# Attention's value products with V stationary, two heads on the two column halves of the array, scaled once per token tile

## The chip, the cores and the metric

The kernel runs on one core of a Trainium2 chip. The metric is the device time of one execution in microseconds (us), the median of several runs. One execution was also recorded by the hardware profiler. The engines are TensorE (PE in the rows; its weight loads PEld), VectorE (DVE), ScalarE (ACT), GpSimd (POOL) and the queue of SyncE (SP), which issues the loads.

## What is computed

Two layers of a diffusion backbone over 256 context tokens and 512 latent tokens of width 1024. Each layer projects the modulated input once, runs three mixers side by side (a gated MLP over tokens, grouped-query attention, a gated DeltaNet in both directions), joins them in one output projection with a post-norm, and ends with a squared-ReLU MLP. The change is in attention: 6 query heads of 64 channels share 2 key and value heads, a latent token sees all 768 tokens, a context token the 256 of the context, and the second layer needs only the latent tokens.

```
def _attend(q, k, v):
    s = jnp.einsum('bqhgd,bkhd->bhgqk', q, k).astype(jnp.float32) * (HEAD_DIM ** -0.5)
    pr = jax.nn.softmax(s, axis=-1).astype(v.dtype)
    return jnp.einsum('bhgqk,bkhd->bqhgd', pr, v)
```

## The kernel before

The kernel is written as streams of steps (Python generators). A planner (`Flow`, with a rough cost of each instruction in `Flow.cost`) decides at build time which stream goes on next; the engines then run what was traced in that order, each engine in order. Every operation is recorded by one helper, so all rows carry line 206, and tiles are told apart by their names.

A layer has three stages. First come the projections: q, k, v for attention, the convolutions of the DeltaNet, the gate z (`z_gate`, which shares the one buffer `axn` with `qk_norm`). Then, in one call of `flow.run`, attention runs beside the DeltaNet: three pairs of heads, each with a chain of 12 scan steps (`dn_scan`: products with `rW`, `rT`, `rK`, then `rQ` and `rA` for the output; each step ends a copy `vn` on ACT), the making of their operands (`gs`, `rW`, `rK`, ...), and the preparation of the third pair (`Lx`, `Xx`, `tm` on DVE). The chains have a head start of 1000 ns (`BIAS`) in the planner's choice, so that attention fills the gaps between their steps. In the first layer `mods` also streams the next modulation weights (`modw`) through PE in this stage. At the end come the output projection (`y`, `yh`, `whi`) and the MLP. The output projection starts after attention in program order, and for each token tile it needs all mixers.

Attention (`attention`, `att_out`) goes over token tiles t of 128 (6 in the first layer, 4 in the second) and 6 heads in each. For a head: the scores are four products of the queries `qs` with the key parts `akh` and `akl` (two for a context tile) into a wide PSUM tile `ax`; DVE takes the row maximum `amx` and scales it to `anm`; ACT takes the exponential `ape` with its row sum, DVE the reciprocal `ars`; PE transposes `ape` in blocks of 128 keys, ACT copies them to `apT`; and for each block of 128 keys c one product with `apT` stationary and the values of both value heads moving adds to a PSUM tile of 128 columns, of which the head uses 64. DVE scales these by `ars` into `aot`. After the sixth head three transposes of `aot` and a copy `ayb` on ACT make the tile channel-major, and ACT's queue issues its store. A head has 6 blocks of keys in a latent tile and 2 in a context tile: 312 products in all, 168 in the first layer and 144 in the second. The scores of a head are traced ahead of the products of the head before.

PSUM tiles are lent out by the planner: four narrow ones of one bank (`mm`) and two wide ones (`ax`). Scans, makes, modulation, transposes and the value products all ask for the four `mm`.

Of the kernel before, what the change touches and what calls it, by code (L numbers as in the profile page):

```python
# [8 lines left out]
F32 = mybir.dt.float32  # L9
# [30 lines left out]
class Flow:  # L40
    """Interleaves streams of work (generators that yield after each step) as they are traced. The engines run what is
    traced in order, so the stream whose last step ends first, by a rough cost of each instruction, goes on next. A stream
    yields a generator to start it, a key to wait until that key is in `done`, a tuple of classes of PSUM tiles to get,
    or the time to go on."""

    # wait for a result of the same engine, of another one
# [14 lines left out]
    def lend(self, cls, tiles):  # L61
        """PSUM tiles for the streams to ask for"""
        self.spare[cls] = [(0.0, i) for i in range(len(tiles))]
        for i, t in enumerate(tiles):
            self.slots[cls, i] = t
# [8 lines left out]
    def cost(self, eng, op, out, ins, kw):  # L74
        n = max([self.width(out)] + [self.width(a) for a in ins])
        if eng == "tensor":
# [5 lines left out]
            return 2.0 * max(35.0 + 0.62 * m, 0.83 * n)  # L82
# [32 lines left out]
    def when(self, s):  # L115
        """the time a stream can go on, None while what it waits for is not there"""
# [11 lines left out]
    def run(self, *gens, side=(), drain=False):  # L128
        """until the streams gens end; those of side go on in the next run if they have not ended, or else with drain"""
# [37 lines left out]
    def step(self, gen, val, ahead):  # L167
        """one step of a stream, its instructions as if they were traced that much earlier"""
# [8 lines left out]
    def aside(self, gen):  # L177
        """starts a stream that need not end with the run"""
        self.start(gen, self.last, False)

    def start(self, gen, now, main, bias=0.0, ahead=0):
        """a stream, or a list of it with the ns and the instructions it has ahead of others"""
# [5 lines left out]
    def drop(self, ap):  # L188
        """gives a PSUM tile back, after the last instruction on it"""
# [21 lines left out]
class _Core:  # L211
    """the engines, with a note of all that is issued to them"""
# [6 lines left out]
def _tb(v):  # L219
    """token tile whose chunks the backward direction takes at step pair v (the forward one takes tile v)"""  # L220
# [63 lines left out]
class K:  # L284
# [22 lines left out]
    def setup(self):  # L307
# [29 lines left out]
        # scratch in DRAM  # L337
# [7 lines left out]
    def store(self, out, in_):  # L345
        """a store, traced when the data is about to be there: loads keep a queue to themselves"""
# [1590 lines left out]
```

## Time and profile before

| | |
|---|---|
| median of 3 runs | 2101.5 us (2100.75 to 2103.27) |
| span of the profiled execution | 2099.3 us, so 2.2 us lie outside the span |
| PE, weight loads, DVE, ACT, POOL busy | 93%, 76%, 65%, 44%, 9% of the span |
| value products, both layers | 624 PE records, 88.4 us busy |
| attention and scans, first layer | about 318 to 575 us of the span |
| attention and scans, second layer | about 1467 to 1668 us of the span |

The page gives the busy share of each engine over the span and in 40 slices. Since the kernel has stages with different limits, the two stretches with attention are read from views limited to them: busy time of each engine by stretch, groups of instructions by shape, and the instructions in order of time. A float32 product on the full array has two records, a transposition one. Records overlap, so the time that a product takes from the next one is read from starts in a dense row: a row that merges n records of one kind lasts n - 1 distances and the length of one record.

### The profile page before, as it was taken

What the parts mean: (1) busy time and instruction counts of PE and PEld (TensorE: products, weight loads), DVE (VectorE), ACT (ScalarE), POOL (GpSimd) and SP (SyncE); (2) the same over time, 40 slices, a digit from 0 to 9 for tenths busy, and PEclk for the clock granted to TensorE, in tenths of its full rate; (3) what the DMA queues carried; (4) which work ended last, traced back from release to release, by engine and by line L of the source; (5) the groups of instructions that cost most, each with busy time, mean ns of one, the idle gap of its engine ahead of it and who ended that gap; (6) DMA issues with size and microseconds to landing.
All of it is one profiled execution on the core that took longest, in us unless ns stands there. A gap on an engine that the chain in (4) does not pass through costs nothing. (4 is left out here: it accounts for less than half of the span.)

```text
span 2099.3 us, 31005 instructions
## 1 busy us (share of the span) xinstructions
PE 1944.5 (93%) x11870; PEld 1601.5 (76%) x11870; DVE 1358.6 (65%) x2659; ACT 921.4 (44%) x1881; POOL 195.3 (9%) x375
## 2 busy tenths in 40 slices
PE   6999779989898999999999989997988889999998
PEld 2887655678777888888888778875877768788886
DVE  5578887865577436362457777889896485544555
ACT  4444346566645322322232265443866445422341
POOL 1111221010012000000000111122100010000001
PEclk8999989989999999999999979977999999999999
DMA  7311024312335424241445243110101434322231
GB/s 280 103 46 51 16 75 149 117 40 64 112 110 181 132 72 159 81 140 43 139 161 173 98 142 95 53 36 26 34 23 30 166 129 164 107 90 81 96 107 59
DMA packets 98240, 208.91 MB, mean 100 GB/s; under 512 B 30850, under 2 KB 45058, under 8 KB 98092
## 3 DMA queue, kind: packets, MB, share of 16 engines
q1 hardware_dynamic: 86956, 189.24, 27.9%
q10 hardware_dynamic: 11136, 17.70, 2.2%
q8 instruction: 93, 1.52, 0.3%
q14 instruction: 55, 0.45, 0.1%
HBM read 184.38 MB, written 17.79 MB: 96 GB/s over the span
## 5 line engine op out<-in xcount | busy, mean ns | idle before, releaser
L206 ACT ACTIVATE whi<-wraw 128x1024 fp32r<-128x1024 f32 (+2 forms) x188 | 194.9, 1050 | 440.6 <-PE ax L206 287.8
L206 DVE TENSOR_TENSOR wlo<-wraw,whi 128x1024 fp32r<-128x1024 f32 (+2 forms) x188 | 226.4, 1211 | 224.6 <-ACT whi L206 224.1
L206 PE MATMUL mm<-x2xh,whi 128*128 128x256 f32 (+1 forms) x832 | 288.4, 347 | 10.5 <-ACT whi L206 9.0
L206 PE MATMUL mm<-x2xh,wlo 128*128 128x256 f32 (+1 forms) x832 | 287.3, 346 | 1.6 <-DVE wlo L206 1.6
L206 PE MATMUL mm<-x2xl,whi 128*128 128x256 f32 (+1 forms) x832 | 287.7, 346 | 0.0
L206 PE MATMUL ax<-whi,hh 128*128 128x512 f32 x640 | 251.2, 392 | 0.0
L206 PE MATMUL ax<-whi,hl 128*128 128x512 f32 x640 | 250.0, 391 | 0.0
L206 PE MATMUL ax<-wlo,hh 128*128 128x512 f32 x640 | 249.9, 390 | 0.0
L206 PEld LDWEIGHTS mm<-x2xh,whi 128*128 128x128 f32 x832 | 158.9, 191 | 34.1 <-ACT whi L206 9.4
L206 DVE TENSOR_TENSOR acc<-acc,ax 128x1024 f32<-128x1024 f32 x68 | 82.9, 1219 | 148.3 <-PE ax L206 148.1
L206 PEld LDWEIGHTS mm<-x2xh,wlo 128*128 128x128 f32 x832 | 158.6, 191 | 22.6 <-DVE wlo L206 2.4
L206 PEld LDWEIGHTS mm<-x2xl,whi 128*128 128x128 f32 x832 | 158.8, 191 | 19.9
L206 PEld LDWEIGHTS ax<-whi,hh 128*128 128x128 f32 x640 | 120.2, 188 | 29.7 <-ACT hh L206 5.2
L206 PEld LDWEIGHTS ax<-whi,hl 128*128 128x128 f32 x640 | 120.1, 188 | 27.5 <-DVE hl L206 2.9
L206 PEld LDWEIGHTS ax<-wlo,hh 128*128 128x128 f32 x640 | 120.2, 188 | 27.0 <-issue 2.6
L206 ACT ACTIVATE rl<-mm 128x256 f32<-128x256 f32 (+1 forms) x104 | 50.7, 490 | 129.1 <-PE mm L206 123.7
L206 DVE SCALAR_TENSOR_TENSOR acc<-modw,cz,acc 128x1024 f32<-128x1024 f32 x80 | 101.2, 1280 | 8.4 <-DMA acc<-in_mod_b 5.4
L206 POOL TENSOR_SCALAR rs<-mv 128x1 f32<-128x1 f32 x52 | 33.1, 637 | 699.1 <-DVE mv L206 696.8
L206 PE MATMUL mm<-ava,apT 128*128 128x128 f32 x624 | 88.4, 285 | 2.7 <-ACT apT L206 1.2
L206 PEld LDWEIGHTS mm<-ava,apT 128*128 128x128 f32 x624 | 78.8, 197 | 7.2 <-ACT apT L206 3.2
L206 DVE TENSOR_TENSOR hl<-rl,hh 128x768 fp32r<-128x768 f32 (+2 forms) x76 | 54.4, 716 | 29.4 <-ACT hh L206 29.4
L206 DVE SCALAR_TENSOR_TENSOR cacc<-cb,cw,cacc 128x772 f32<-128x772 f32 (+1 forms) x72 | 69.7, 972 | 0.7 <-ACT cacc L206 0.2
(255 smaller groups left out, 4178.5 us busy)
## 6 DMA issues: line engine op xcount, KB each, us to landing
wraw<-in_w_up SPq DMA_DIRECT2D x64, 512.0 KB
wraw<-in_w_down SPq DMA_DIRECT2D x64, 512.0 KB
modw<-in_mod_w SPq DMA_DIRECT2D x56, 512.0 KB
modw<-in_mod_w SPq DMA_DIRECT2D x80, 256.0 KB
wraw<-in_w_ch SPq DMA_DIRECT2D x22, 512.0 KB
wraw<-in_w_out SPq DMA_DIRECT2D x16, 512.0 KB
x_d<-xt ACTq DMA_DIRECT2D x16, 512.0 KB
xt<-x_d SPq DMA_DIRECT2D x14, 512.0 KB
```

The source lines that it names most:

```text
L206: return f(*args, **kw)
```

## The change

- The stationary and the moving operand of the value product change places: the values of one value head (128 keys by 64 channels) are stationary and the transposed probabilities `apT` move, so that the result is channel-major [64 channels, 128 tokens]. Two heads, one of each value head, are taken together, and their products alternate between the two column halves of the array (output partitions 0 to 63 and 64 to 127). The heads go in the order `HEADS`, the odd one of a pair traces the products of both, and the second `apT` lies in the buffer of `akT`, which is free by then.
- All heads of a token tile add up in one PSUM tile of 384 columns (`st["po"]`), taken at the second head and given back after the tile's last instruction.
- The scaling by the reciprocal of the row sums is done once for the tile: one reciprocal of 6 columns, six small products that spread it over 64 partitions (`ars` broadcast stationary, the identity moving), a copy `abc` on ACT, and one product of 128x384 on DVE into `ayb`. The 60 scalings into `aot`, the 60 reciprocals and the 30 transposes of `aot` go away.
- The factor 1/8 moves from the exponential to `qs`; the maximum is taken negated, so that `anm` needs no instruction of its own.
- The planner counts a float32 product with 64 output rows at half its former cost, and `z_gate` waits in the planner for the stream that used its buffer before.

```diff
-            return 2.0 * max(35.0 + 0.62 * m, 0.83 * n)
+            return (1.0 if m == 64 else 2.0) * max(35.0 + 0.62 * m, 0.83 * n)
...
+HEADS = (0, 3, 2, 5, 4, 1)
...
+        yield f"z{l}{t - 1}" if t > self.tiles[0] else f"qk{l}{LT[-1]}"
...
+                nc.vector.tensor_reduce(out=nm, in_=ps, axis=AX.X, op=ALU.max, negate=True)
...
-        pT = ap_.tile([P, TOK], F32, tag="apT", bufs=1, name="apT")
+        pT = st["pT"][m % 2]
...
-        po = yield from self.psum(P)
+        if m % 2 == 0:
+            self.flow.signal(f"po{l}{i}")
+            return
+
+        if m == 1:
+            st["po"] = yield from self.psum(384)
+        pv = st["po"].rearrange("p (a q) -> p a q", a=3)
         for c in range(kts):
-            nc.tensor.matmul(po, pT[:, c * P : c * P + P], va[:, c].rearrange("p a b -> p (a b)"), start=(c == 0), stop=(c == kts - 1))
-        yield
-        nc.vector.tensor_scalar(out=st["ot"][:, h, :], in0=po[:, HD * (h // 3) : HD * (h // 3) + HD], scalar1=st["rs"][:, h : h + 1], scalar2=None, op0=ALU.mult)
-        self.drop(po)
+            for e in range(2):
+                h = HEADS[m - 1 + e]
+                nc.tensor.matmul(
+                    pv[_half(h % 2), h // 2, :], va[:, c, h // 3, :], st["pT"][e][:, c * P : c * P + P],
+                    start=(c == 0 and m == 1), stop=(c == kts - 1), skip_group_check=True,
+                )
...
+        rs = self.small([P, NH], "ars")
+        nc.vector.reciprocal(rs, st["su"])
+        yield
+        pb = yield from self.psum(384)
+        for h in range(NH):
+            nc.tensor.matmul(
+                pb[_half(h % 2), h // 2 * P : h // 2 * P + P], rs[:, h : h + 1].broadcast_to([P, HD]), self.ident, start=True, stop=True
+            )
...
+        nc.scalar.copy(bc, pb)
...
+        nc.vector.tensor_tensor(out=y, in0=pv, in1=bc.rearrange("p (a q) -> p a q", a=3), op=ALU.mult)
+        self.drop(st["po"])
```

What PE runs in a row, first where attention is alone at the end of the first layer's stage. Before, one head's cycle is its six value products (`ava`), four transposes, the scores of the next head, two transposes:

```order
L206 MATMUL mm_69<-ava,apT 128x128 x6
L206 MATMUL mm_66<-c_ident,ape 128x128 x4
L206 MATMUL ax_71<-akh,qs 128x512
L206 MATMUL ax_71<-akl,qs 128x512
L206 MATMUL ax_71<-akh,qs 128x256
L206 MATMUL ax_71<-akl,qs 128x256
L206 MATMUL mm_68<-c_ident,ape 128x128 x2
L206 MATMUL mm_67<-ava,apT 128x128 x6
```

Now the end of a token tile there (the two narrow rows at the top are the last of twelve that alternate between `apT` and `akT`):

```order
L207 MATMUL mm_69<-apT,ava 64x128
L207 MATMUL mm_69<-akT,ava 64x128
L207 MATMUL ax_71<-akh,qs 128x512
L207 MATMUL ax_71<-akl,qs 128x512
L207 MATMUL ax_71<-akh,qs 128x256
L207 MATMUL ax_71<-akl,qs 128x256
L207 MATMUL mm_67<-c_ident,ars 64x128 x6
L207 MATMUL mm_66<-c_ident,ape 128x128 x4
```

Two heads now have one run of narrow products between the full-width ones, and the spreading of `ars` is a second short run per tile.

In the middle of the stage, beside the scans of the third pair. Before, a head's products stand mostly in one piece between the products of a scan step (`S`, `rr`, `vn`):

```order
L206 MATMUL mm_68<-ava,apT 128x128 x6
L206 MATMUL mm_67<-c_ident,gs 128x128 x2
L206 MATMUL mm_66<-rr,rT_2737 128x128 x2
L206 MATMUL mm_69<-c_ident,ape 128x128 x4
L206 MATMUL mm_68<-S,rQ_2747 128x128
L206 MATMUL mm_66<-vn,rK_2742 128x128 x2
```

Now:

```order
L207 MATMUL mm_69<-akT,ava 64x128
L207 MATMUL mm_69<-apT,ava 64x128
L207 MATMUL mm_67<-vn,rK_2700 128x128 x2
L207 MATMUL mm_68<-vn,rA_2710 128x128 x2
L207 MATMUL mm_69<-akT,ava 64x128
L207 MATMUL ax_71<-akh,qs 128x512
L207 MATMUL ax_71<-akl,qs 128x512
L207 MATMUL mm_66<-S,rW_2742 128x128 x2
```

The narrow products of a pair are cut by full-width ones here, so that the array changes between the two shapes more often. Over the whole kernel the 312 narrow value products stand in 75 runs and the 60 products of `ars` in 15, with 160 places at which a product of another shape stands next to them.

On DVE, at the end of the first layer's stage. Before, each head has a reduction, two small scalings and a reciprocal:

```order
L206 TENSOR_REDUCE amx<-ax_70 128x1
L206 TENSOR_SCALAR anm<-amx 128x1
L206 TENSOR_SCALAR aot<-mm_66,ars 128x64
L206 RECIPROCAL ars<-asu 128x1
L206 TENSOR_REDUCE amx<-ax_71 128x1
```

Now the head has the reduction alone, and the tile one reciprocal and one wide product:

```order
L207 SCALAR_TENSOR_TENSOR qs<-aqT,qs 64x3x128 x2
L207 RECIPROCAL ars<-asu 128x6
L207 TENSOR_REDUCE anm<-ax_71 128x1
L207 TENSOR_TENSOR o<-o,crn 128x768
L207 TENSOR_TENSOR ayb<-mm_69,abc 128x384
```

What moved is the place of attention's heads among the scan steps. In the first layer 12, 8 and 16 heads had their exponential before step 24, between steps 24 and 36 of the scans, and after; now 11, 12 and 13. In the second layer it was 14, 8 and 2 in the order of the instructions, and now 12, 10 and 2.

## Rows read from the trace of the kernel before

**Rows 1.** The page: span, and busy time of each engine.
```profile
span 2099.3 us, 31005 instructions
PE 1944.5 (93%) x11870; PEld 1601.5 (76%) x11870; DVE 1358.6 (65%) x2659; ACT 921.4 (44%) x1881; POOL 195.3 (9%) x375
```

**Rows 2.** Busy times of the engines in six stretches (start:end, length, then as headed).
```profile
core 0: us, PE busy (x) PEld busy (x) DVE busy (x) ACT busy (x) POOL busy (x), PEclk, DMA share, GB/s
318.00:455.00 137.00, 131.01 (x1059) 90.08 (x1058) 102.89 (x373) 81.08 (x264) 8.55 (x22) 0.95 0.34 103
455.00:515.00 60.00, 55.77 (x427) 51.28 (x427) 37.89 (x130) 41.37 (x141) 2.48 (x2) 0.97 0.16 44
515.00:575.00 60.00, 53.42 (x408) 48.39 (x406) 30.99 (x78) 38.05 (x95) 2.47 (x2) 1.00 0.39 128
1467.00:1584.00 117.00, 104.61 (x1133) 93.45 (x1133) 105.20 (x358) 84.87 (x243) 9.84 (x37) 0.97 0.11 27
1584.00:1644.00 60.00, 52.88 (x429) 47.32 (x428) 34.59 (x121) 38.03 (x119) 1.83 (x2) 1.00 0.19 55
1644.00:1668.00 24.00, 17.81 (x114) 15.60 (x112) 7.18 (x20) 9.88 (x35) 1.83 (x2) 0.86 0.51 180
```

**Rows 3.** ACT on tile `ape` in these stretches: length, busy (records, two a head).
```profile
318.00:455.00 137.00, 6.78 (x24) 0.95 0.34 103
455.00:515.00 60.00, 7.93 (x16) 0.97 0.16 44
515.00:575.00 60.00, 15.71 (x32) 1.00 0.39 128
1467.00:1584.00 117.00, 13.88 (x28) 0.97 0.11 27
1584.00:1644.00 60.00, 6.94 (x14) 1.00 0.19 55
1644.00:1668.00 24.00, 2.85 (x6) 0.86 0.51 180
```

**Rows 4.** PE by time, attention alone: start us, us, line, operation, shapes, count.
```profile
540.29 1.60 PE L206 MATMUL mm<-ava,apT 128*128 128x128 f32 x12
541.73 0.60 PE L206 MATMUL mm<-c_ident,ape 128*128 128x128 f32 x4
...
543.10 1.57 PE L206 MATMUL mm<-ava,apT 128*128 128x128 f32 x12
```

**Rows 5.** PE by time, products of 64 columns of the gated MLP.
```profile
96.75 2.38 PE L206 MATMUL mm<-gws,gv 128*64 128x128 f32 x40
```

**Rows 6.** PE by time, where the shape of the products changes.
```profile
1517.89 0.38 PE L206 MATMUL mm<-c_ident,gs 128*128 128x128 f32 x2
1518.20 0.68 PE L206 MATMUL ax<-kq 64*64 64x128 f32 x16
1518.81 0.71 PE L206 MATMUL mm<-S,rW 128*128 128x128 f32 x4
1519.36 0.61 PE L206 MATMUL mm<-S,rQ 128*128 128x128 f32 x4
```

**Rows 7.** Groups by shape: busy us, mean ns, idle before and its releaser.
```profile
L206 DVE TENSOR_SCALAR aot<-mm,ars 128x64 f32<-128x64 f32 x60 | 16.9, 282 | 26.1 <-PE mm L206 25.2
L206 DVE RECIPROCAL ars<-asu 128x1 f32<-128x1 f32 x60 | 9.6, 160 | 12.6 <-ACT ape L206 12.2
L206 DVE TENSOR_SCALAR anm<-amx 128x1 f32<-128x1 f32 x60 | 8.8, 147 | 0.7
L206 DVE SCALAR_TENSOR_TENSOR zth<-zth,mm 128x384 f32<-128x384 f32 x10 | 5.5, 548 | 1.0 <-ACT zth L206 1.0
L206 DVE TENSOR_TENSOR qs<-aqT,qs 64x384 fp32r<-64x384 f32 x20 | 11.1, 553 | 0.6
L206 ACT COPY ayb<-mm 128x384 f32<-128x384 f32 x10 | 4.8, 478 | 7.7 <-PE mm L206 7.7
L206 ACT ACTIVATE zth<-mm 128x384 f32<-128x384 f32 x10 | 4.9, 494 | 4.7 <-DMA z_d<-zth 4.7
```

More of the change, by code (lines that the diff above doesn't have):

```diff
@@ L1058, in attention @@
                 a, b = _half(h2), _half(1 - h2)
-                nc.scalar.activation(out=qs[a, :, h2, :], in_=qT[a, :, sl], func=AF.Copy)
-                nc.vector.tensor_tensor(out=qs[b, :, h2, :], in0=qT[a, :, sl], in1=qs[a, :, h2, :].bitcast(F32), op=ALU.subtract)
+                nc.scalar.activation(out=qs[a, :, h2, :], in_=qT[a, :, sl], func=AF.Copy, scale=0.125)
+                nc.vector.scalar_tensor_tensor(
+                    out=qs[b, :, h2, :], in0=qT[a, :, sl], scalar=0.125, in1=qs[a, :, h2, :].bitcast(F32), op0=ALU.mult, op1=ALU.subtract
+                )
             yield
-            st = {"rs": self.small([P, NH], "ars"), "ot": ap_.tile([P, NH, HD], F32, tag="aot", bufs=1, name="aot")}
-            for h in range(NH):
+            st = {"su": self.small([P, NH], "asu"), "pT": (ap_.tile([P, TOK], F32, tag="apT", bufs=1, name="apT"), kT)}
+            for m, h in enumerate(HEADS):
                 q = qs[:, h // 2, h % 2, :]
@@ L1073, in attention @@
                     yield late
-                mx = self.small([P, 1], "amx")
-                nc.vector.tensor_reduce(out=mx, in_=ps, axis=AX.X, op=ALU.max)
                 nm = self.small([P, 1], "anm")
-                nc.vector.tensor_scalar(out=nm, in0=mx, scalar1=-0.125, scalar2=None, op0=ALU.mult)
+                nc.vector.tensor_reduce(out=nm, in_=ps, axis=AX.X, op=ALU.max, negate=True)
                 yield
-                i = NH * t + h
+                i = NH * t + m
                 if i - NH * self.tiles[0] > 1:
@@ L1106, in att_out @@
             yield
-        po = yield from self.psum(P)
-        for c in range(kts):
-            nc.tensor.matmul(po, pT[:, c * P : c * P + P], va[:, c].rearrange("p a b -> p (a b)"), start=(c == 0), stop=(c == kts - 1))
-        yield
-        nc.vector.tensor_scalar(out=st["ot"][:, h, :], in0=po[:, HD * (h // 3) : HD * (h // 3) + HD], scalar1=st["rs"][:, h : h + 1], scalar2=None, op0=ALU.mult)
-        self.drop(po)
+        if m % 2 == 0:
[4 more added lines that the diff above has]
+        pv = st["po"].rearrange("p (a q) -> p a q", a=3)
+        for c in range(kts):
+            for e in range(2):
[4 more added lines that the diff above has]
+                )
         self.flow.signal(f"po{l}{i}")
         yield
-        if h < NH - 1:
+        if m < NH - 1:
             return
-        ot = st["ot"].rearrange("p h e -> p (h e)")
-        pt = yield from self.psum(384)
-        for a in range(3):
-            self.tr(pt[:, a * P : a * P + P], ot[:, a * P : a * P + P])
+        rs = self.small([P, NH], "ars")
[5 more added lines that the diff above has]
+                pb[_half(h % 2), h // 2 * P : h // 2 * P + P], rs[:, h : h + 1].broadcast_to([P, HD]), self.ident, start=True, stop=True
+            )
+        yield
+        bc = ap_.tile([P, 384], F32, tag="abc", bufs=1, name="abc")
+        nc.scalar.copy(bc, pb)
+        self.drop(pb)
         yield
         y = ap_.tile([P, 3, P], F32, tag="ayb", bufs=1, name="ayb")
-        nc.scalar.copy(y, pt.rearrange("p (a b) -> p a b", a=3))
-        self.drop(pt)
+        nc.vector.tensor_tensor(out=y, in0=pv, in1=bc.rearrange("p (a q) -> p a q", a=3), op=ALU.mult)
+        self.drop(st["po"])
         yield from self.store(self.y_d[l, t, :, 2:5, :], y)
```

11 lines of the change are left out of this document (4 added, 7 removed).

## The prediction

> **What bounds the kernel now.** The page first: PE is busy 93% of a span of 2099.3 us, DVE 65% [rows 1]. That is a mean over stages, so the second view is the busy time by stretch, for the two stages that hold attention [rows 2]. From 318 to 455 us PE is busy 131.0 of 137 us: scans of two pairs, the modulation's products and attention fill it. From 455 to 515 (the third pair's scan) it is busy 55.8 of 60, and from 515 to 575, where attention is alone but for the third pair's gate, 53.4 of 60. In the second layer DVE is as full as PE from 1467 to 1584 (105.2 and 104.6 of 117 us), since the third pair's preparation runs there. Then PE leads (52.9 of 60), and the last 24 us are waits: no engine is busy for more than 17.8. A busy PE is not a saturated one, so the third view counts what the work is: 12, 8 and 16 heads in the first layer's stretches, 14, 7 and 3 in the second's [rows 3]. The fourth is one cycle of a head where attention is alone [rows 4]: 2.81 us from one block of value products to the next (540.29 to 543.10), of which the products take 1.44. PE is never idle in it; this end of the first stage is bound by PE.
>
> **The products themselves.** Before, 12 records take 1.44 us, 0.24 us for each of 312 products [rows 4]: 74.9 us. The 30 transposes of `aot` go at a distance of 0.11 us (the four of [rows 6] in `S,rQ` last 0.61, the two of `gs` 0.38): 3.3 us. Removed: 78.2 us of PE. For a product of 64 columns that alternates between the halves the gated MLP has the row: 40 records in 2.38 us [rows 5], less the length of one (0.38 - 0.11 = 0.27), over 39 distances, is 0.054 us a record and 0.108 a product. It has the same stationary and moving shape as the new product, but adds nothing up. Added: 312 + 60 products at 0.108, 40.2 us. By this alone PE saves 38.0 us.
>
> **The changes of shape.** The new order has 160 borders between these narrow products and others. What a border costs is in [rows 6]. The last of two `gs` starts at 1518.00, the first `kq`, a narrower shape, at 1518.20: 0.20 instead of 0.11, 0.09 lost on the way in. On the way out the last `kq` starts at 1518.61 (its row ends at 1518.88, one length later) and `S,rW` at 1518.81: 0.09 lost again, and then the four records of `S,rW` last 0.71 instead of the 0.61 of `S,rQ` behind them: 0.10 more. And a run of two alternating halves begins and ends with one half alone, one record of 0.11. A run costs 0.39 us beside its products, a border 0.20, 160 borders 32 us. The other narrow shapes (modulation, preparation) get 17 borders fewer, at about 0.14: 2.4 us back. PE saves 38.0 - 32 + 2.4, some 8 us; bounds are 38 (borders hidden in time in which PE waits anyway) and a loss of 15 (each border also delays a scan step that PE works on next). The Trainium skill, TensorEngine Tiling (Array Packing), section Tiling Modes, says that a change of tiling mode, unlike one of tile within a mode, drains the engine. The trace agrees, with 0.20 against 0.11; without the rule the sum would be the 38 us above.
>
> **DVE and ACT.** DVE loses 60 scalings, reciprocals and `anm` at 0.282, 0.160 and 0.147 us, 35.3 us [rows 7]. It gains 10 reciprocals (0.16) and 10 products of 128x384 out of PSUM, nearest to `zth` at 0.548: 7.1 us. `qs` keeps shape and count (0.553). So 16.9 us go in the first layer and 11.3 in the second. They count only where DVE ends last, from 1467 to 1584. The new product waits for the copy `abc` on ACT; behind it on DVE stand `rr` and `S` of the scans, for up to 0.48 us ten times, hidden where a scan step waits longer than that. ACT swaps the copy `ayb` for `abc` of the same size (0.478 [rows 7]), so nothing. In the first stage's end ACT is busy 38.05 us for 16 heads [rows 2, 3], 2.38 a head, and doesn't get less: that is a floor for the new cycle.
>
> **By stretch.** The new cycle where attention is alone: two heads need 2 x (2.81 - 1.44) for scores and transposes, 12 x 0.108 and one run at 0.39, 4.43 us, so 2.22 a head; the products of `ars` add (6 x 0.108 + 0.39) / 6 = 0.17. That is 2.39, next to ACT's 2.38. Beside the scans the mean run has 312/75 = 4.2 products, so 12 come in three runs: 2 x 0.39 more for two heads, 2.78 a head. A context head goes from 0.94 (scores 0.24, transposes 0.22, products 0.48) to about 1.04.
> - 318 to 455: 6 context and 6 latent heads, 22.5 us of PE, become 6 and 5, 6 x 1.04 + 5 x 2.78 = 20.1. PE bounds: -2.4.
> - 455 to 515: 8 heads become 12, 22.5 become 33.4. PE's idle 4.2 us take part of it: +7.
> - 515 to 575: 16 x 2.81 = 45.0 and 15 us of other work and waits. Now 13 x 2.39 = 31.1 and the same 15: -14.
> - 1467 to 1584: 14 heads become 12. DVE saves 14 x 0.589 and two maxima; PE saves 39.3 - 33.4: -7.
> - 1584 to 1644: 7 become 10, 19.7 become 27.8, with 7.1 us idle on PE: +3.
> - 1644 to 1668: 3 become 2, beside the third pair's gate, which the output projection needs: -3.
>
> Sum: -16 us. The work behind, projection and MLP, is bound by PE and starts that much sooner, so nothing in it takes the gain back.
>
> **The rest.** The planner's halved cost and the wait in `z_gate` only reorder the projections. ACT waited 4.7 us there for the store of z that frees the buffer [rows 7], which can go; a worse order can cost as much. I take 0. The buffer of `akT` is written long after its last reader. Loads, stores and the queues of SP and POOL stay; a tile's store still goes through ACT's queue, after the DVE product instead of the copy.
>
> **The rivals.**
> - *Borders are free.* Where they fall into waits, all 38 us of PE count: 2063 us. For it, PE leaves 24 us idle in the middle stretches of both layers [rows 2]; against it, the borders stand in the busy ones too. The Trainium skill, TensorEngine Tiling (Array Packing), section Theoretical Speedup, gives up to 2x for 64 columns; [rows 5] agree for a long run.
> - *The saving is hidden.* Scans wait for their own chain, and what PE and DVE save becomes idle time: 2101 us. For it, the stretches with scans have PE and DVE waiting on each other; against it, the end from 515 on has no scan.
> - *Slower: one PSUM tile fewer.* Attention now holds one of the four `mm` from a tile's second head to its end, where it held one for the products alone. Two scan chains, makes and transposes share three. If each of 72 scan steps waits for one more return of a tile, at the copy of 0.478 us that empties one [rows 7] 34 us are added to -16: 2119 us; it decides from 16/72 = 0.22 us a step on. The Trainium skill, Perfetto Trace Analysis, section Optimization Strategy, says that repeated gaps on the engine that should be full can mean too little PSUM; no row shows a wait for a tile yet.
> - *The halves don't overlap* when both add up in one bank: 312 more distances of 0.108, 34 us, against -16: 2119 us. [Rows 5] speak against it.
>
> **How the numbers follow.** The forecast is -16 us on the profiled execution, 2083.3 us of span; the median of the runs is 2.2 us above the span, so 2085.5 us. Chances: forecast 0.57 (own range 2072 to 2096), free borders 0.15, hidden 0.10, PSUM 0.14, no overlap 0.04. The range reaches to the free borders below (2062) and, above, into the PSUM case where only half of its steps wait (2106). Faster by more than 0.2% (4.2 us, about what a measurement of this kernel can tell): 0.57 + 0.15 = 0.72. Same: 0.10. Slower: 0.18.
>
> **What would show it.** In the trace after: 12 narrow products in one run in about 1.4 us (2.7 if the halves don't overlap); 0.20 us between starts at a border; DVE about 28 us less busy; some 2.4 us a head in the first stage's end, and that stage ending about 9 us sooner, the second's 7 more. Wrong I would be if a step of the third pair's scan, 60/12 = 5.0 us now, takes over 6.3: 24 steps of 1.3 us are twice the forecast's gain.

## The result and the profile after

| | before | after |
|---|---|---|
| median (runs) | 2101.1 us (2099.3 to 2103.3, 4) | 2120.1 us (2114.2 to 2125.9, 4) |
| ratio, 95% interval | | 1.0094 (1.0073 to 1.0114) |
| profiled execution, its span | 2101.5, 2099.3 us | 2125.9, 2123.9 us |

The changed kernel is 0.9% slower; forecast were 2085.5 us and a range of 2062 to 2106. The recorded execution is the slowest of the four, 5.9 us above the median.

The page after, the two lines that answer to [rows 1]:

```profile
span 2123.9 us, 31022 instructions
PE 1952.7 (92%) x11960; PEld 1592.9 (75%) x11960; DVE 1339.7 (63%) x2499; ACT 922.1 (43%) x1881; POOL 195.3 (9%) x375
```

PE was to lose 8 us and has 8 more. The stretches of [rows 2], bounded by the same scan steps (start:end, length, busy time of each engine, granted clock):

```profile
325.00:462.00 137.00, 125.54 (x955) 82.31 (x954) 98.24 (x334) 76.63 (x255) 7.63 (x16) 0.97 0.33 104
462.00:535.00 73.00, 68.55 (x604) 57.76 (x603) 41.11 (x118) 50.77 (x159) 2.51 (x2) 0.94 0.18 49
535.00:587.00 52.00, 44.50 (x388) 35.96 (x387) 20.51 (x31) 32.78 (x85) 2.47 (x2) 0.90 0.38 130
1490.00:1601.00 111.00, 100.06 (x892) 84.36 (x892) 92.08 (x289) 74.48 (x221) 5.53 (x12) 0.93 0.10 23
1601.00:1671.00 70.00, 64.83 (x607) 53.66 (x607) 35.85 (x110) 44.99 (x132) 1.84 (x2) 0.90 0.16 40
1671.00:1689.00 18.00, 10.50 (x105) 8.76 (x103) 4.91 (x10) 8.73 (x32) 1.83 (x2) 0.82 0.22 69
```

and ACT on `ape` in three of them (two records a head, so 12, 13 to 14 and 10 heads), beside [rows 3]:

```profile
462.00:535.00 73.00, 11.41 (x24) 0.94 0.18 49
535.00:587.00 52.00, 12.94 (x27) 0.90 0.38 130
1601.00:1671.00 70.00, 9.93 (x20) 0.90 0.16 40
```

The lengths of [rows 2] were 137, 60, 60, 117, 60 and 24. They changed by 0, +13, -8, -6, +10 and -6 us, together +3, where -2.4, +7, -14, -7, +3 and -3 were forecast. So five of the six signs hold (the first stretch didn't change), but the scan stretches paid more and the first layer's tail gave less. The span grew by 24.6 us; nearly 22 of them lie outside these stretches, mostly in the projections, for which the forecast took 0: from the first convolution (`cacc`) to the first `akh` 195.2 became 199.9 us in the first layer and 168.2 became 175.0 in the second, and the piece ahead of it in the second layer, from the end of the MLP, 72.5 became 79.0.

### The profile page after: what moved, and what is told of

It is laid out like the page before. It is cut to its first block, busy times and chain, and to the rows that moved or that the text cites. A ratio compares the mean times of both kernels' runs of the same rounds, so it can differ in the third digit from the quotient of the medians.

```text
span 2123.9 us, 31022 instructions
## 1 busy us (share of the span) xinstructions
PE 1952.7 (92%) x11960; PEld 1592.9 (75%) x11960; DVE 1339.7 (63%) x2499; ACT 922.1 (43%) x1881; POOL 195.3 (9%) x375
## 4 chain that ended last, share of the span: by engine, by line
PE 65%; DVE 16%; ACT 6%; issue 5%; POOL 4%; DMA 4%; SPq 0%; ACTq 0%; POOLq 0%; DVEq 0%
PE mm L207 41%; PE ax L207 24%; DVE cacc L207 2%; DVE wlo L207 2%; DVE tm L207 2%; DVE Xx L207 1%; POOL crn L207 1%; DVE M L207 1%; DVE A L207 1%; DMA wraw<-in_w_out 1%; POOL rs L207 1%; DVE axn L207 1%; DMA wraw<-in_w_up 1%; DVE st L207 1%; DMA modw<-in_mod_w 1%
## 5 line engine op out<-in xcount | busy, mean ns | idle before, releaser
L207 PE MATMUL mm<-whi,yh 128*128 128x512 f32 x160 | 64.8, 415 | 10.7 <-ACT whi L207 9.3
L207 DVE TENSOR_REDUCE anm<-ax 128x1 f32<-128x768 f32 (+1 forms) x60 | 50.7, 847 | 36.2 <-PE ax L207 35.9
L207 ACT ACTIVATE v<-mm,sh,sc 128x128 f32<-128x128 f32 x152 | 58.2, 463 | 29.3 <-PE mm L207 24.5
```

Source lines behind the costliest of these rows:

```text
L207: return f(*args, **kw)
```

## What the narrow products do in the trace

PE after, by time, where attention is alone (the run in question starts at 563.71):

```profile
562.76 0.43 PE L207 MATMUL mm<-apT,ava 128*64 128x128 f32 x2
563.13 0.66 PE L207 MATMUL mm<-c_ident,ape 128*128 128x128 f32 x4
563.71 0.32 PE L207 MATMUL mm<-akT,ava 128*64 128x128 f32 x1
563.72 0.32 PE L207 MATMUL mm<-apT,ava 128*64 128x128 f32 x1
563.87 0.27 PE L207 MATMUL mm<-akT,ava 128*64 128x128 f32 x1
563.88 0.27 PE L207 MATMUL mm<-apT,ava 128*64 128x128 f32 x1
...
564.85 0.38 PE L207 MATMUL mm<-akT,ava 128*64 128x128 f32 x2
565.17 0.50 PE L207 MATMUL ax<-akh,qs 128*128 128x512 f32 x1
```

The two halves start 0.01 us apart and a pair of records every 0.11: they do overlap while they add up in one bank. The run has eleven products (22 records) and takes 563.71 to 565.17, 1.46 us. The twelfth of the pair stands alone ahead of it, at 562.76, and takes 0.37 us with two borders of its own. A run of all twelve, of which this order has few (one starts at 537.69), takes 1.46 us too, about the 1.4 that was forecast. The border price shows best around the spreading of `ars` between two products of a scan step:

```profile
516.35 0.71 PE L207 MATMUL mm<-rr,rT 128*128 128x128 f32 x4
516.99 0.88 PE L207 MATMUL mm<-c_ident,ars 128*64 128x128 f32 x12
517.80 0.71 PE L207 MATMUL mm<-vn,rK 128*128 128x128 f32 x4
```

Four full records take 0.44 to the next start in a dense row; here it is 0.64, 0.20 late. Half of that isn't the border's: the row of `rT` itself lasts 0.71, where four records last 0.61, so 0.10 was lost at its own start. Twelve narrow records would take 0.65 and take 0.81, and `rK` lasts 0.71 as well. 0.10 + 0.16 + 0.10 is 0.36 us for a run beside its products, where the forecast had 0.39, or 0.18 a border.

DVE's side came as forecast: `aot`, `anm` and 60 small reciprocals are gone (35.3 us), and these two are new, 10 x 0.19 and 10 x 0.55 us:

```profile
L207 DVE RECIPROCAL ars<-asu x10: 184/191/192, 441.4 to 1676.9; 128x6 f32<-128x6 f32 x10
L207 DVE TENSOR_TENSOR ayb<-mm,abc x10: 543/550/558, 447.5 to 1682.2; 128x384 f32<-128x384 f32 x10
```

That is 27.9 us of records less; the page shows only 18.9 less, since it counts time once where records overlap.

## The experiments

Each was timed beside the kernel before on the same chip. The ratio to it, with its interval, is what is compared; "us" below are medians, and differences are taken to the kernel before of the same session (2100.7 to 2102.7 us).

**The planner's two edits.** e1 and e2 take them out of the changed kernel, e3 and e4 put them into the kernel before.

```diff
 e1, e2, e4: the full price
-            return (1.0 if m == 64 else 2.0) * max(35.0 + 0.62 * m, 0.83 * n)
+            return 2.0 * max(35.0 + 0.62 * m, 0.83 * n)
 e1: z_gate without the wait (e3 and e4 have it)
-        yield f"z{l}{t - 1}" if t > self.tiles[0] else f"qk{l}{LT[-1]}"
```

> The changed kernel with the planner's cost of a 64-row product back at the full price and without the wait in z_gate: only attention's own change is left. In the profile the 24.6 us that the changed kernel lost lie in the projections before attention (+7.1 in the first layer, +13.0 in the second) and not in attention's stages (+1.3 together). Theory A (the two planner edits reorder the projections, and that is the loss): the projections go back to about 195.2 and 173.6 us from the first convolution to the first akh, and the time to 2120 - 20 = about 2100 us. Theory B (the loss is attention's own, through what it holds in PSUM and where its products stand; the projections only moved with it): stays at about 2119 us.

> The changed kernel with the full planner's cost, but with the wait in z_gate kept. Theory A1 (the wait is what makes the projections longer): stays near 2119 us and the projections keep about +20. Theory A2 (the halved cost does it): about 2100 us, like the kernel without both. Theory B: 2119 us for all of them.

> The kernel before with the two planner edits alone, attention as it was. The halved cost then touches the DeltaNet's products with 64 rows and the gated MLP's. Theory A: the projections get about 20 us longer, 2101 + 20 = 2121 us. Theory B: 2101 us.

> The kernel before with the wait in z_gate alone. Theory A1 (the wait): about 2121 us. Theory A2 (the halved cost): 2101 us. Theory B: 2101 us.

| | attention before | attention changed |
|---|---|---|
| neither edit | 1 | 1.0016 (1.0004 to 1.0029), e1 |
| the wait | 0.9976 (0.9961 to 0.9991), e4 | 0.9984 (0.9973 to 0.9994), e2 |
| the wait and the halved price | 1.0036 (1.0022 to 1.0050), e3 | 1.0094 (1.0073 to 1.0114), the change |

The wait alone gains 5.7 and 7.8 us, the halved price loses 14 and 22. With the wait and the full price, attention's own change costs 2.6 us (2099.1 against 2096.5); the two intervals overlap, so it may be nothing. So theory A2 holds for the price; A1, that the wait does harm, falls; and attention's 16 us of gain are not there either.

**Whose price.** e7 halves the price for attention's products alone, e11 for these and `kq`.

```diff
-            return (1.0 if m == 64 else 2.0) * max(...)
+            return (1.0 if m == 64 and ("ava" in ins[0].tensor.name or "ars" in ins[0].tensor.name) else 2.0) * max(...)
```

> The changed kernel, but the planner's halved cost holds for attention's value products and the products of ars alone; the 64-row products of the DeltaNet and of the gated MLP have the full price again. Theory D (the loss of the halved cost comes from the products it wasn't meant for, which reorder the projections): about 2099 us, like with the full cost. Theory E (attention's cheaper price puts its heads where they delay the scans): 2115 to 2120 us.

> The changed kernel, with the planner's halved cost for attention's products and for the 288 products of keys and queries in the DeltaNet's preparation (kq), and the full price for the gated MLP's and the gates' products. With the halved cost for all it took 2120 us, with attention's alone 2099 us. If the price of the preparation's products causes the loss: about 2120 us, with the projections of the second layer some 10 us longer. If the gated MLP's and the gates' products cause it: about 2099 us.

e7 took 2099.0 us (0.9987, 0.9975 to 1.0000), like the full price; e11 2112.4 (1.0065, 1.0042 to 1.0087). Of the 22 us some 14 come with the price of the DeltaNet's `kq`, the rest with the gated MLP's and the gates' products. From the products that the edit was about comes none that can be seen. (Each of these kernels is one order, so the division is a rough one.) The second layer up to the first `akh`, e7 and then the changed kernel (the end of the MLP to the first convolution, then to `akh`):

```profile
1214.68:1285.99 71.31, 60.21 (x395) 52.93 (x394) 49.18 (x124) 51.41 (x96) 13.84 (x25) 0.86 0.41 135
1285.99:1456.40 170.41, 156.08 (x1046) 131.92 (x1044) 144.82 (x296) 68.57 (x111) 29.52 (x31) 0.89 0.14 45
```

```profile
1227.14:1306.14 79.00, 68.42 (x426) 60.72 (x425) 49.20 (x125) 51.90 (x97) 14.23 (x25) 0.83 0.41 132
1306.14:1481.16 175.02, 154.12 (x1114) 131.21 (x1112) 152.92 (x318) 74.16 (x119) 32.10 (x59) 0.86 0.13 44
```

In the first piece the changed kernel has PE busy 8 us longer, with 31 more records, and 8 us more of time. In the second, 68 more PE records and 22 more of DVE, preparation taken in sooner, but PE is busy for less of it and idle 6.6 us longer: its waits for `wlo` and `PB` of DVE went from 7.1 to 12.3 us. Part of that comes back later (from `akh` to scan step 24 125.4 became 120.3 us), the rest doesn't. The first layer loses as much: 6.3 us up to `akh` and 5.9 from there to the output projection.

One mechanism was not tested apart: the granted clock, which is lower in both rows of the changed kernel. Over its four runs it is 0.946 on the mean, over ten of e7 0.955. In the 102 runs of the kernel before that were timed beside the experiments, 0.001 less of clock goes with 0.84 us more of time; by that, an estimate, some 7 of the 22 us came with the clock, and more in the recorded execution, whose clock was 0.941. e2 has less than e4 too (0.956, 0.961); 3.7 us would go with that, more than the 2.6 between them. Whether a lower clock made the time or the same waits made both isn't shown.

**The held PSUM tile.** e5 holds it in the kernel before, e6 gives it back in the changed one (a tile for each pair of heads, copied by DVE, and no `abc`).

```diff
 e5, on the kernel before with the wait
+        if h == 1:
+            st["hold"] = yield from self.psum(384)
         po = yield from self.psum(P)
...
+        self.drop(st["hold"])
 e6, on the changed kernel with the full price and the wait
-            st["po"] = yield from self.psum(384)
+        po = yield from self.psum(P)
...
+        for e in range(2):
+            h = HEADS[m - 1 + e]
+            nc.vector.tensor_copy(y[_half(h % 2), h // 2, :], po[_half(h % 2)])
+        self.drop(po)
```

> The kernel before with the wait in z_gate (2096.5 us) and one edit: attention takes a narrow PSUM tile at the second head of a token tile and gives it back at the tile's end, without using it; no instruction is added. Theory P (holding the tile is what attention's change loses): with the modulation's tile also held, the planner leaves attention without a tile behind the scans; attention has no exponential from about 340 us to the modulation's end near 430, as in the changed kernel with the full cost, and the stretch from the first akh to scan step 36 grows from 194.8 to about 215 us, 20 us more, some of which the tail gives back: about 2110 us. Theory B (the borders between the shapes lose it): no change, 2096 us.

> The changed kernel with the full cost and the wait (2099.1 us), but each pair of heads has its own PSUM tile for its products alone; DVE copies its two halves to ayb (60 copies of 64x128 more, at about 0.28 us 17 us of DVE), the scaling is done in place, and the copy abc goes away. The narrow products and borders stay. Theory P: the stretch from the first akh to scan step 36 in the first layer falls from 215.0 to about 200 us, attention goes on beside the modulation, and the time falls to about 2085 us. Theory B: stays near 2099 us or, with the DVE copies, a little over.

e5 took 2120.5 us (1.0094, 1.0072 to 1.0115): 25 us more than e4, without one instruction more. ACT on `ape` from 340 to 420 us, e4 and then e5:

```profile
340.00:420.00 80.00, 2.27 (x8) 1.00 0.43 125
```

```profile
340.00:420.00 80.00, 0.00 (x0) 1.00 0.41 121
```

Four heads have their exponential there in e4 and none in e5. By the code, the modulation holds one tile of four, attention another, and the chains with their head start ask first for the other two. The changed kernel with the full price (e2) has none there either. But e6, which gives the tile back and has five heads there, took 2098.7 us (0.9993, 0.9979 to 1.0007), the same as e2. Its copies cost DVE 17 us more. So the starvation is real, but it costs nothing that can be seen in the changed kernel, and that e5's 25 us come from it isn't shown: from `akh` to step 36 it lost 13.8 us (194.8 to 208.7), less than the 20 of theory P, and the tail, which was to give some back, lost 5.1.

**The borders.** e8 and e9 keep a pair's products together, by taking the key blocks from the last one and by an earlier trace priority; e8 in e2, with the tile held, e9 in e6. e10 joins the spreading of `ars` to the pair's run.

```diff
-        for c in range(kts):
-            for e in range(2):
+        at = self.tc.cur_priority
+        self.tc.cur_priority = top = max(0, at - 300)
+        for c in reversed(range(kts)):
+            for e in (1, 0):
...
+        self.tc.cur_priority += at - top
 e10, ahead of the last line
+        for e in (1, 0):
+            f = _half(HEADS[m - 1 + e] % 2)
+            nc.tensor.matmul(pb[f], rs[:, e : e + 1].broadcast_to([P, HD]), self.ident, start=True, stop=True)
```

> The changed kernel with the full cost and the wait (2099.1 us), with the products of a pair in reverse order of the key blocks, so that the first one needs the last copy, and with a trace priority 300 instructions earlier: the narrow products stand in 42 runs instead of 84 (22 of 12 products), 84 borders fewer. The tile is held as before. Theory B (borders cost PE 0.20 us each and PE bounds): 17 us of PE less, 2082 us. Theory P (attention starves for a tile in the middle, where PE waits anyway): only the borders of the tails and of the second layer count, some 5 to 8 us, 2092 us, and the first layer's stretch to step 36 stays near 215 us.

> The kernel with a PSUM tile of its own for each pair (2098.7 us, 140 borders, no starved attention), with the key blocks in reverse order and the products traced 300 instructions earlier: 45 runs, 90 borders. Theory B (PE bounds the stages, a border costs it 0.20 us): 50 borders less, 10 us, 2089 us. Theory H (beside the scans PE waits for the scans' own chain, so what attention saves there becomes idle time of PE): PE busy falls by about 10 us, PE's idle time in attention's stages rises by about as much, and the time stays within 2096 to 2101 us.

> Like the one with a tile for each pair and unbroken runs, but the two products that spread the reciprocals stand in the pair's own run and tile; ACT copies 128 columns of them (30 copies), DVE scales the pair's halves out of PSUM into ayb (60 products of 64x128, which were copies before), and the tile's own run of ars and its product go away: 31 runs, 62 borders, 23 of the runs of 14 products. Theory B: 78 borders less than 140, 16 us, about 2083 us. Theory H: 2095 to 2101 us, with PE less busy and more idle.

| | borders | us | ratio |
|---|---|---|---|
| e2, then e8 | 168, 84 | 2099.1, 2103.3 | 1.0014 (1.0002 to 1.0027) |
| e6, then e9 | 140, 90 | 2098.7, 2100.6 | 0.9999 (0.9986 to 1.0012) |
| e10 | 62 | 2107.2 | 1.0030 (1.0018 to 1.0042) |

Fewer borders bring no time; e8 and e10 lie above both of their forecasts. On the pages PE's busy time falls by 7.4 us from e2 to e8 (1935.3 to 1927.9), where 17 were forecast, and by 3.0 from e6 to e9 (1932.2 to 1929.2), where 10 were. The tail of the first layer (after scan step 36), e2 and e8:

```profile
527.60:576.60 49.00, 44.91 (x424) 36.54 (x422) 22.14 (x33) 35.95 (x92) 2.47 (x2) 1.00 0.49 158
```

```profile
525.80:580.50 54.70, 43.94 (x423) 35.69 (x421) 21.70 (x34) 34.86 (x91) 2.59 (x2) 0.97 0.43 141
```

PE has the same records and is busy 1.0 us less, but idle 10.8 us instead of 4.1. Its waits for `ape` grew from 0.5 to 4.9 us, and 2.3 us for `qs` and 0.5 for the copy `apT` came in: whole runs were bought with waits, though few of these are for the last copy itself.

**The pieces of the change in the old kernel.** All stand on e12, the kernel before with the wait and the negated maximum (the factor 1/8 goes to `qs`).

```diff
 e12
-                nc.vector.tensor_reduce(out=mx, in_=ps, axis=AX.X, op=ALU.max)
-                nc.vector.tensor_scalar(out=nm, in0=mx, scalar1=-0.125, scalar2=None, op0=ALU.mult)
+                nc.vector.tensor_reduce(out=nm, in_=ps, axis=AX.X, op=ALU.max, negate=True)
 e13: two heads' products together, in the old form
+        if h % 2 == 0:
+            return
+        for g in (h - 1, h):
+            po = yield from self.psum(P)
 e14: channel-major, full width; e15 the same with 64 columns
+            nc.tensor.matmul(po, va[:, c].rearrange("p a b -> p (a b)"), pT[:, c * P : c * P + P], ...)
+            nc.tensor.matmul(po[_half(h % 2)], va[:, c, h // 3, :], pT[:, c * P : c * P + P], ...)
 e16: att_out2 is the pair form of e9
+            pair = t >= self.tiles[-1] - 1 + l
+                late = (self.att_out2 if pair else self.att_out)(l, t, m, n // P, pe, va, st)
```

> The kernel before with the wait in z_gate (2096.5 us) and the maximum taken negated, the factor 1/8 in qs: 60 small scalings of 0.147 us less on DVE, 8.8 us, PE untouched. The prediction counted DVE's savings in the second layer where DVE is the fullest engine: 24 x 0.147 = 3.5 us, 2093 us. If DVE's savings are hidden there too: 2096.5 us.

> The kernel before with the wait and the negated maximum (2088.8 us), and the value products of two heads traced together behind the second of them, in the old token-major form of full width; the second head's probabilities lie in the buffer of akT as in the changed kernel. Nothing is added or left out, no narrow shape, no tile is held. Theory J (taking two heads together is what loses the 10 us between this kernel and the changed one: no product of the first head to fill PE with, then a block of two heads before a scan step): about 2099 us. Otherwise 2089 us.

> The kernel before with the wait and the negated maximum (2088.8 us), and the value products channel-major with V stationary, head by head, in full width (both value heads stationary, half of the output used, 312 products of the old duration); DVE copies a head's half to ayb (60 copies of 64x128 for 60 scalings), the scaling comes once per tile through the products of ars, and the 30 transposes go. No pairs, no held tile, only the 20 borders of ars. If the channel-major form itself or the scaling per tile loses the 10 us: about 2099 us. If the pairs (J) or the narrow shape (B) do: 2087 to 2090 us.

> Like the channel-major kernel in full width, but each head's products have 64 columns on one half of the array, head by head, so that the halves don't overlap (a product keeps 0.22 us) and 188 borders come in. Against the full width it tells the price of the shape alone: theory B (0.20 us a border on a bound PE): 168 borders more, 34 us more. Theory H (PE has slack beside the scans, and the borders count only in the tails): 5 to 10 us more.

> The kernel before with the wait and the negated maximum (2088.8 us); the last two token tiles of the first layer and the last of the second, which stand at the stages' ends, have the paired narrow products in unbroken runs with a PSUM tile for each pair, the other tiles the old form. If the narrow form is worth its saving only where PE is alone with attention (2.81 us a head before, 2.4 after): 12 and 3 heads there, 6 to 7 us, about 2082 us. If the pairs lose as much there: 2089 us.

| | us | ratio |
|---|---|---|
| e12 | 2088.8 | 0.9949 (0.9936 to 0.9963) |
| e13 | 2093.3 | 0.9957 (0.9939 to 0.9975) |
| e14 | 2106.4 | 1.0022 (1.0009 to 1.0035) |
| e15 | 2136.6 | 1.0168 (1.0145 to 1.0191) |
| e16 | 2089.3 | 0.9938 (0.9918 to 0.9959) |

e12 gains 6.2 us on e4, where 3.5 were expected, and is 0.5% faster than the kernel before; it and e16 are the best two here. But the gain isn't where it was expected: in the traces the second layer's stage, from `akh` to the output projection, became 2.2 us longer (211.0 to 213.1), the first's 6.7 shorter (259.5 to 252.9), and the last MLP, which the edit doesn't touch, 4.1 shorter (343.6 to 339.5, from its first product with the hidden layer `hh`). e13 took neither of its two times, and its interval overlaps that of e12: a loss of 10 us by pairs (J) isn't there. e15 against e14 puts the narrow shape alone into the whole: 30.2 us more. By the traces e14 has 32 borders (the runs of `ars` are cut in places) and e15 188, so 0.19 us for each of 156, near the 0.18 of the rows; PE's busy time rises by 22.4 us, 0.14 each. Theory H, 5 to 10 us, falls by that; but the two orders differ as well, so the price isn't free of their difference. By time, 12 records of a head in e14 and, below, in e15:

```profile
560.18 1.58 PE L206 MATMUL mm<-apT,ava 128*128 128x128 f32 x12
561.60 0.60 PE L206 MATMUL mm<-c_ident,ape 128*128 128x128 f32 x4
```

```profile
565.03 1.52 PE L206 MATMUL mm<-apT,ava 128*64 128x128 f32 x12
566.48 0.50 PE L206 MATMUL ax<-akl,qs 128*128 128x512 f32 x1
```

1.42 and 1.45 us to the next start: on one half alone, 64 columns are no faster than 128. e16's two tails became 4.5 and 7.3 us shorter than e12's, as hoped, but the second one's was given back in the output projection (94.7 for 87.4 us, to the first product with `hh`), and the last MLP from there on took 343.6 us as in the kernel before (343.3), where e12 had 339.5. That e14 loses 16.4 us on e12 no theory foresaw.

**What an order alone is worth.** Since the pieces didn't add up, e17 and e18 change nothing but the planner's head start, in e2 and in e12.

```diff
-BIAS = 1000.0
+BIAS = 500.0
```

> The changed kernel with the full cost and the wait (2099.1 us), with the chains' head start in the planner 500 ns instead of 1000: no instruction is added, left out or changed, the planner only comes to another order (attention goes first more often). Theory R (differences of up to some 10 us between these kernels are those of two orders and belong to no part of the edit): the time moves by 5 us or more in this kernel or in the one with the same edit below, and not in the same direction or size. If an order is worth little: both stay within 3 us. If attention starves by the chains' head start (P): this one gains, some 10 us, and the kernel before with the negated maximum, which doesn't starve, doesn't.

> The kernel before with the wait and the negated maximum (2088.8 us), with the chains' head start 500 ns instead of 1000, as a second sample of what another order of the same instructions is worth. Theory R: 5 us or more away from 2088.8, in either direction. Else 2086 to 2092 us.

2121.5 us (1.0094, 1.0077 to 1.0111) and 2120.1 (1.0086, 1.0071 to 1.0101): 22 and 29 us more than e2 and e12, by the order alone. The pages of e12 and e18:

```profile
span 2085.2 us, 30970 instructions
PE 1927.6 (92%) x11870; PEld 1594.1 (76%) x11870; DVE 1353.5 (65%) x2599; ACT 924.8 (44%) x1881; POOL 195.7 (9%) x375
```

```profile
span 2120.3 us, 30961 instructions
PE 1943.5 (92%) x11870; PEld 1604.8 (76%) x11870; DVE 1348.8 (64%) x2599; ACT 926.3 (44%) x1881; POOL 197.7 (9%) x375
```

The count of instructions that each engine works on is the same; the span isn't. With the new order the first layer's way from `akh` to scan step 24 takes 184.0 instead of 136.9 us, and the tail 24.2 instead of 64.5. Every edit in this kernel re-plans all of it, so a difference of some 20 us between two of these kernels can belong to their orders. Of theory R the first half holds, that an order is worth 5 us and more. The second doesn't: both kernels moved in the same direction and by nearly the same, so a smaller head start is worse as such, and the two aren't samples of a random scatter. What edits that only re-plan moved here runs from nothing (e7 against e2) over 6 to 8 us (the wait) and 14 and 22 (the price) to 25 (e5) and these 22 and 29. So the 2.6 us of attention's own change, e13's 3.4 and e14's 16.4 can't be put down to a part of an edit; that they are the order's isn't shown either. And theory P's forecast falls: with the smaller head start attention is asked sooner, but nothing was gained.

## Why the prediction was wrong, point by point

From 2085.5 to 2120 us are 34.6. Some 16 of them come with the planner's two edits (22 for the price, less 6 for the wait) and 19 with attention's own change, which was to gain 16 us and cost 2.6. So two steps failed.

- **The products, the overlap of the halves, the border** were sized right: 0.054 us a record, a run of twelve in 1.46 us, 0.18 us a border in the rows and 0.14 to 0.19 in e15 against e14. The rival that the halves don't overlap is out.
- **"The planner's halved cost and the wait in `z_gate` only reorder the projections. I take 0"** is the first step that failed. The price costs 22 us (14 in the kernel before) and the wait gains 6 to 8; both do nothing but reorder. The only bound that I gave, 4.7 us from one wait of ACT, was the size of one cover, not of an order. The edit also reached products that it wasn't meant for (`kq`, the gates, the gated MLP), which the diff showed: any product with 64 output rows.
- **"455 to 515: 8 heads become 12 ... PE's idle 4.2 us take part of it: +7"** is the second, and so is the +3 of "1584 to 1644": the overlap. +13 and +10 came. Of the forecast's 16 us only some 6 were less work for PE; 9 were idle time that the added heads were to fill, 4 of 4.2 us here and 5 of 7.1 there. In the stretches above PE is still idle for 4.4 and 5.2 us, so under 2 were filled. In e2, without the price and with two heads more in each, 3.2 were. The work itself was sized nearly right: added up from start to start, attention's products took 9.5 us more here, where 10.9 were forecast, and 8.3 there, where 8.1 were. On top came other products, mostly of the third pair's preparation (`zs`, `PA`, `PB`) and of the scan. The growth stands in one step each, the first of the third pair (from the copy `vn` of step 24 to that of step 25), before and then after:

```profile
455.05:461.45 6.40, 5.88 (x47) 5.23 (x45) 4.91 (x17) 5.67 (x27) 0.00 (x0) 1.00 0.27 84
1584.50:1594.60 10.10, 8.20 (x80) 6.81 (x79) 3.82 (x14) 8.50 (x33) 0.07 (x1) 1.00 0.20 50
```

```profile
462.58:478.71 16.13, 15.41 (x163) 12.35 (x156) 7.62 (x19) 12.03 (x43) 1.08 (x2) 0.74 0.14 29
1601.70:1621.86 20.16, 16.78 (x223) 14.18 (x220) 7.37 (x20) 14.57 (x43) 1.84 (x2) 0.69 0.20 49
```

  The other eleven steps take 56.9 us for 53.3 and 49.5 for 49.4. In the long steps lie the exponentials of three heads for one before, more of the preparation, and a granted clock of 0.74 and 0.69 for 1.00. With the price halved for attention alone (e7) the two steps take 4.2 and 9.5 us, with that of `kq` too (e11) 15.5 and 18.8: so the price reordered attention's stages as well, and not the projections only.
- **"PE saves ... some 8 us"** was nearly lost on the way. From e4 to e2 PE's busy time fell from 1936.6 to 1935.3 us. From start to start, idle time left out, the value products fell from 76.1 to 52.6 us and the 4.0 of the transposes of `aot` went; but the products of `ars` take 10.0, and those of the scans, of `gs` and of the scores, beside which the runs now stand, 16 more. What of these 16 is the borders' price and what the lower clock (0.955 for 0.962) wasn't told apart.
- **The tail, -14 in the first layer,** came as -8. With the full price it came whole: from e4 to e2 the way from step 36 to the output projection went from 64.7 to 49.0 us, with 15 heads in it for 17. In the changed kernel two things took from it. A head's cycle is 2.63 us, where 2.39 were forecast (six heads from 563.71 to 579.50, one `ars` among them): most pairs have two runs, with the first product alone. And the tail is broken once, where the third pair's gate falls into it:

```profile
547.31 0.55 DVE L207 TENSOR_TENSOR ayb<-mm,abc 128x384 f32<-128x384 f32 x1
548.01 0.40 PE L207 MATMUL mm<-apT,ava 128*64 128x128 f32 x2 [1.69 <-DVE ayb L207]
550.74 0.79 PE L207 MATMUL ax<-akh,qs 128*128 128x512 f32 x1 [0.93 <-ACT o L207]
554.53 1.12 PE L207 MATMUL mm<-c_ident,ape 128*128 128x128 f32 x4 [2.15 <-ACT ape L207]
```

  (start, length, instruction, in brackets the idle time before it and its releaser). PE waits 1.69 us for the tile's one product on DVE, which stands behind `o`, a product that itself waited for the gate; then for the wide PSUM tile that the gate used, then for the next `ape`. The forecast had named what stands on DVE behind the new product, not what it stands behind. But the break's idle time isn't new. The tail before has as much at its gate:

```profile
526.74 0.87 PE L206 MATMUL ax<-c_ident,zg 128*128 128x128 f32 x6 [2.26 <-DVE zg L206]
532.53 0.87 PE L206 MATMUL mm<-c_ident,ape 128*128 128x128 f32 x6 [2.40 <-ACT ape L206]
```

  What is new is the clock behind it (last section): 10.2 us at the lower level, in which PE was busy for 7.1. At the higher level these would be some 3.5 less, an estimate from half the clock.
- **The second tail, -3, "so nothing in it takes the gain back":** it became 6 us shorter, but the output projection behind it longer: 67.2 us for 56.6 to the first product of the MLP, 95.3 for 86.6 to the first with its hidden layer (`hh`). Waits up to the latter, before and after (us, times, longest):

```profile
ACT whi L206 <- DMA wraw<-in_w_out: 7.7, 5, 2.4
PE mm L206 <- ACT whi L206: 6.0, 2, 4.0
```

```profile
ACT whi L207 <- DMA wraw<-in_w_out: 13.0, 8, 3.9
PE mm L207 <- ACT whi L207: 10.9, 5, 5.0
```

  SP issues the first of these loads at 1658.55 before, 10.9 us ahead of the first product, and at 1684.60 after, 4.9 ahead: the loads didn't move with the tail. So PE waits 4.9 us longer for weights, about half of what was given back; 3.0 more are a wait for `yl`, which the kernel before doesn't have.
- **DVE** lost what was forecast. Where it was said to count (1467 to 1584) the stretch became 6 us shorter, for 7. That this is DVE's saving isn't shown: in e12, with 8.8 us less on DVE, the same stretch became 8.7 us shorter (127.1 to 118.4), and the next took 11.4 back (59.2 to 70.6).
- **The rivals.** The PSUM rival gave 2119 us, and 2120 came, but that is a coincidence. It had each scan step pay for a missing tile; the step of the third pair's scan that was named as a sign is 73/12 = 6.1 us on the mean, under the 6.3, and what grew is one step in twelve. The tile starves attention instead, and giving it back gained nothing. "Hidden", 0.10 in the forecast, fits the time of attention's own change (2099.1 against 2096.5), but not by its way either: PE's idle time in attention's stages is 53.8 us in e4 and 55.2 in e2, so next to nothing of the saving became idle time.

What stays open: how much of the price's 22 us is the clock's and what made it fall, why e14 loses 16.4 us, and why the held tile costs 25 us in one kernel and nothing in the other. Differences of orders are large enough for the last two; that they are the cause wasn't shown.

## What to carry to other kernels

Where a planner sets the order, an edit to its prices is a change of its own: limit it to the products that it is about, and time it apart from the rest (here 22 us, more than all of attention's change). Before a few microseconds are put down to an edit, time the same instructions in one or two other orders; here that alone moved 22 and 29 us. Idle time of an engine beside a chain of steps isn't room for more work: here 9 us of it were counted as filled and under 2 were. And the granted clock belongs beside each time that is compared.

## What was not expected of the hardware

The granted clock fell in the broken tail. Windows of 5 us of the changed kernel (length, busy time of PE, PEld, DVE, ACT and POOL, then the granted clock):

```profile
545.00:550.00 5.00, 2.75 (x20) 1.74 (x19) 2.29 (x3) 1.45 (x4) 1.40 (x1) 0.94 0.12 41
550.00:555.00 5.00, 2.11 (x6) 1.63 (x7) 1.82 (x2) 2.20 (x4) 0.00 (x0) 0.50 0.35 98
555.00:560.00 5.00, 5.00 (x33) 4.27 (x31) 0.96 (x1) 2.31 (x6) 0.00 (x0) 0.54 0.85 308
```

PE was busy for 4.9 of 10 us, and the clock stood at 0.50, the lower of its two levels (1.2 and 2.4 GHz), in the second half of them and at 0.54 in the 5 us behind, though PE was busy all through these. At 550.74 the score product of 512 columns took 0.79 us; at 565.17 it took 0.50. The clock stood at the lower level from 549.4 to 559.6 us. The tail before has a like stretch at its gate and kept the higher one:

```profile
524.00:534.00 10.00, 5.34 (x41) 4.69 (x39) 5.68 (x12) 5.21 (x11) 0.70 (x1) 1.00 0.50 162
```

PE was busy for 5.3 of 10 us there. What decided between the two isn't shown.
